# A transformer block with a 16,384-expert layer: routing without casts and spread wider, GpSimd on a third of u's lower parts, and v's last two groups by column halves

## The chip, the cores and the metric

The kernel runs on one core of one Trainium2 chip, with its engines TensorE (PE), VectorE (DVE), ScalarE (ACT), GpSimd (POOL) and the DMA queues that SyncE (SP), ACT and POOL feed. The metric is the device time of one execution in microseconds (us). The median of three executions is 2597.5 us (2593.54 to 2606.66). Lower is better.

## The reference, cut to what matters

One block of a diffusion transformer on 256 tokens of width 2048 in float32: a token mixer (differential attention and gated linear attention, in the first half of the time, which the diff does not touch), and then the PEER layer, a sparse layer of 16,384 experts:

```python
def peer_ffn(h, wq, keys, u, v):
    q = (h @ wq).reshape(B, T, PEER_HEADS, 2, PEER_DQ // 2)             # 8 heads, 2 halves of 128
    s = jnp.einsum('bthpd,hpkd->bthpk', q, keys)                        # 128 keys for each half
    s1, i1 = lax.top_k(s[..., 0, :], PEER_TOPK)                         # 16 best of each half
    s2, i2 = lax.top_k(s[..., 1, :], PEER_TOPK)
    cand = (s1[..., :, None] + s2[..., None, :]).reshape(B, T, PEER_HEADS, 256)
    cidx = (i1[..., :, None] * PEER_NKEYS + i2[..., None, :]).reshape(B, T, PEER_HEADS, 256)
    top_s, pos = lax.top_k(cand, PEER_TOPK)
    idx = jnp.take_along_axis(cidx, pos, axis=-1)
    g = jax.nn.softmax(top_s, axis=-1)
    ...
        act = jax.nn.gelu(jnp.einsum('pd,ped->pe', xb, u[ib]), approximate=False)
        return jnp.einsum('pe,ped->pd', act * gb, v[ib])
```

u and v are 16384 x 2048 tables (134 MB each in float32). The output is x plus a gate times this layer.

## The kernel before, in words

**Products.** TensorE multiplies in float32r, so that every float32 weight block of 128 x 1024 (0.524 MB by its shape) is split in two: `hi`, a rounded copy that ACT makes (L90, tile `whi`), and `lo`, the rest, a subtraction `raw - hi` (L92, tile `wlo`) that either DVE or POOL makes. The class `Stream` (object `W`) walks over one long list of blocks: SP loads them ahead into `wraw` buffers (L76), `split_to` makes `hi` and `lo` up to 3 blocks ahead of the products, and `W.share(s)` says for block `s` whether POOL makes `lo` (else DVE). Instructions of one engine run in the order in which they are written.

**Dense and sparse part of the PEER layer.** For 192 of the 256 tokens (TD) the layer is computed densely: all 128 groups of 128 experts are multiplied (u), a weight matrix `A` built from the routing masks out the experts that were not chosen, and a second pass multiplies by v. For the last 64 tokens (NS), 64 gathers of 128 rows of u (128 x 2048 float32, 1.05 MB by its shape), and later 64 of v, are fetched by indirect DMAs that POOL issues (L1163, tile `gat`, 2 buffers), and DVE multiplies them (L1170 with `hrow` in PSUM for u, L1185 for v).

**Jobs.** Everything beside the products is written as generators in lanes of `Jobs`. The product loops call `jobs.tick()`, and a generator that yields n goes on n ticks later. In the product with u (`experts_in`) a tick comes every four pairs of matmuls (a *pair* is L1219 with `hi` and L1220 with `lo`; a group of experts has 16 pairs, all of u has 2048), and a block is used up every 8 pairs. In the product with v a tick comes every 5 matmuls.

**The order of the stages that the diff touches.**
- *Queries* (w_q, 32 blocks, from 1151 us on): q = h @ wq, scores, and the job `route`. `route` runs 16 rounds (8 heads, 2 halves of the tokens); a round finds the 16 best of each half (`best16`: MAX, MAX_INDEX and MATCH_REPLACE on DVE), adds them to 256 candidates, finds the 16 best of these, and turns their positions back into expert numbers (L1070 to L1080). Its yields are 1, 1, 2, 1, 2, so a round takes 7 ticks. Seven rounds and a part of the eighth are written among the products of the queries, the rest among those of u.
- *u, routing* (from 1253 us): the rest of `route`, then `weigh` (softmax). POOL makes `lo` of three blocks in four.
- *u, gains*: the job `gains` builds `A` in 48 steps of 4 ticks. The lane `sparse` does one gather and one multiplication of an earlier gather every 6 ticks, from the start of `gains` on. DVE makes all `lo` (`W.share` is always false from here to the end). Finished groups are parked in DRAM, since `A` does not exist yet: 36 pairs of groups.
- *u, fetch*: the parked groups come back (SP, tile `back`, one every 3 ticks) and are multiplied into `A` by DVE (L1258); the rest of the groups go straight to `A` (L1248).
- *v* (from 1973 us): 128 groups of 20 matmuls, into PSUM tiles `ya[0..3]` (128 tokens) and `yb[0..3]` (64 tokens, two halves stacked). The last group finishes one column quarter n after the other, and each is at once turned into output: DVE multiplies and adds, TensorE folds `yb` with one more matmul (L1355) that waits for DVE, and SP stores.

Of the kernel before, what the change touches and what calls it, by code (L numbers as in the profile page):

```python
# [7 lines left out]
F32 = mybir.dt.float32  # L8
# [3 lines left out]
AF = mybir.ActivationFunctionType  # L12
OP = mybir.AluOpType
# [12 lines left out]
TD, NS = 192, 64  # L26
# [109 lines left out]
def block_kernel(ctx, tc, a, out):  # L136
# [15 lines left out]
    for m in range(16):  # L152
        if m + NGA < 16:
# [4 lines left out]
    on_pool |= set(range(len(blocks), len(blocks) + 32))  # L158
    blocks += ([a["w_q"][i] for i in (0, 2, 1, *range(3, 32))] + [a["u"][i] for i in range(256)]
               + [a["v_rows"][i * 128:(i + 1) * 128, q * 1024:(q + 1) * 1024] for i in range(128) for q in range(2)])  # L160
# [879 lines left out]

    def score(h, q):
# [10 lines left out]

    def route(h, s):
        for b in (1, 0):
            v = tk.tile([128, 2, 16], F32, name="v", bufs=2)
            iu = tk.tile([128, 2, 16], U32, name="iu", bufs=2)
            il = tk.tile([128, 2, 16], F32, name="il", bufs=2)
            for i in range(2):
                best16(v[:, i], iu[:, i], s[:, 2 * b + i])
                yield 1  # L1060
# [6 lines left out]
            yield 2  # L1067
            pu = tk.tile([128, 2, 16], U32, name="pu", bufs=2)
            pf = tk.tile([128, 2, 16], F32, name="pf", bufs=2)
            V.tensor_scalar(pu[:, 0], pos, 4, None, op0=OP.logical_shift_right)  # L1070
            V.tensor_scalar(pu[:, 1], pos, 15, None, op0=OP.bitwise_and)
            V.tensor_copy(pf, pu)
            S.activation(il, iu, AF.Copy)
            oh = tk.tile([128, 2, 16, 16], F32, name="oh", bufs=1)
            ohf = oh.rearrange("p i k a -> p (i k) a")
            V.tensor_tensor(ohf, pf.rearrange("p i k -> p (i k)")[:, :, None].to_broadcast([128, 32, 16]),
                            io16[:, None, :].to_broadcast([128, 32, 16]), OP.is_equal)
            yield 1
            V.tensor_tensor(oh, oh, il[:, :, None, :].to_broadcast([128, 2, 16, 16]), OP.mult)
            V.reduce_sum(I12[:, b, :, 16 * h:16 * h + 16], oh, axis=AX.X)  # L1080
            yield 2
# [68 lines left out]
    nwq = W.s  # L1150
# [15 lines left out]
    def sparse_in(pool, n, wait):  # L1166
        for j in range(64 + n):
# [5 lines left out]
            yield wait  # L1173
# [115 lines left out]
    with tc.tile_pool(name="gpool", bufs=1, side="right") as pool:  # L1289
        while A is None or any(jobs.lanes.get("gains", ())):  # L1290
            if A is None and not any(jobs.lanes.get("route", ())):
# [3 lines left out]
                jobs.add("sparse", sparse_in(spool, 2, 6))  # L1295
                W.share = lambda s: False
# [32 lines left out]

    part(0)  # L1330
    for i in range(128):
        if i % 2 == 0 and i + 2 < 128:
            part(i + 2)
        t = parts[i // 2 * 2][:, i % 2]
        h0, h1, hb = t[:, 0:128, 0], t[:, 0:128, 1], t[:, 128:TD].rearrange("p t i -> p (t i)")
        for n in range(4):
            if n % 2 == 0:
                hi, lo = W.next()
            c = slice((n % 2) * 512, (n % 2) * 512 + 512)
            first, last = i == 0, i == 127  # L1340
            PE.matmul(ya[n], h0, hi[:, c], start=first, stop=False)  # L1341
            PE.matmul(ya[n], h1, hi[:, c], start=False, stop=False)  # L1342
            PE.matmul(yb[n], hb, hi[:, c], start=first, stop=False)  # L1343
            PE.matmul(ya[n], h0, lo[:, c], start=False, stop=last)  # L1344
            PE.matmul(yb[n], hb, lo[:, c], start=False, stop=last)  # L1345
            jobs.tick()
            if last:
                d = slice(n * 512, n * 512 + 512)
                o = pool.tile([128, 512], F32, name="o", bufs=2)
                V.tensor_tensor(o, ya[n], g2r[:, d], OP.mult)  # L1350
                V.tensor_tensor(o, o, x2r[0][:, d], OP.add)
# [111 lines left out]
```

## Time and profile before

| | |
|---|---|
| Median of 3 executions | 2597.5 us |
| Profiled execution: its own time | 2595.49 us |
| Profiled execution: span from first to last instruction | 2593.7 us |
| Busy in the span: PE, DVE, ACT, POOL | 94%, 76%, 50%, 26% |
| DMA: mean rate over the span | 261 GB/s |
| Queries / product with u / product with v (us from the span's start) | 1151 to 1253 / 1253 to 1973 / 1973 to 2594 |

A busy TensorE only says that matmuls were in flight. The granted clock (PEclk) is a share of 2.4 GHz, and a stretch between 0.5 and 1 was run partly at 1.2 GHz. All times below are counted from the span's start.

### The profile page before, as it was taken

The page shows a single profiled execution, that of the slowest core. Times are in us where ns is not written, and L with a number is a line of the kernel's source. Part 1 is how long each engine was busy: PE and PEld are TensorE (multiplying, and loading weights), DVE is VectorE, ACT ScalarE, POOL GpSimd, SP SyncE. Part 2 cuts the span into 40 slices and gives each one's busy share as a digit, 9 for nine tenths or more (in the row PEclk, how much of TensorE's full clock was granted, in tenths as well). Part 3 has the DMA queues.
Part 4 walks back from the last instruction along what each step waited for, and adds up shares of the span by engine and source line. Part 5 has one row for each costly group of instructions (what it writes and reads, how often), then busy time and mean ns, then how long its engine had stood idle before and what let it go on. Part 6 is the DMA issues. An engine that isn't in the chain of part 4 may idle for free.

```text
span 2593.7 us, 39672 instructions
## 1 busy us (share of the span) xinstructions
PE 2434.1 (94%) x15236; PEld 2190.2 (84%) x15236; DVE 1974.8 (76%) x2609; ACT 1298.6 (50%) x1963; POOL 685.8 (26%) x334
## 2 busy tenths in 40 slices
PE   6799999999999999979779999999999999999998
PEld 3477888888899999979778999989998888888885
DVE  4868888577865665459996888889976888888765
ACT  5453444333344444443336999854554444444442
POOL 4541111212202342147444121222210332322100
PEclk8799999999999999989889999999999999999999
DMA  8665555366647776665456999999997999999973
GB/s 296 221 230 178 182 192 186 122 219 203 212 139 246 256 246 228 199 186 184 129 161 217 325 328 330 328 380 387 394 349 242 367 378 382 365 377 381 334 248 126
DMA packets 195406, 678.07 MB, mean 261 GB/s; under 512 B 21776, under 2 KB 53104, under 8 KB 178064
## 3 DMA queue, kind: packets, MB, share of 16 engines
q1 hardware_dynamic: 155232, 521.50, 58.2%
q0 software_dynamic: 19008, 137.44, 13.5%
q10 hardware_dynamic: 20976, 16.61, 2.1%
q8 instruction: 119, 1.95, 0.3%
q14 instruction: 71, 0.58, 0.1%
HBM read 660.44 MB, written 11.29 MB: 259 GB/s over the span
## 4 chain that ended last, share of the span: by engine, by line
PE 71%; DVE 17%; DMA 5%; issue 2%; ACT 2%; POOL 1%; SPq 0%; ACTq 0%; DVEq 0%; POOLq 0%
PE acc L1219 11%; PE acc L212 6%; PE acc L214 6%; PE acc L213 6%; PE acc L1220 5%; PE yb L1345 5%; PE ya L1341 5%; PE ya L1342 5%; PE ya L1344 5%; PE yb L1343 5%; DVE wlo L92 3%; DMA back<-park 3%; PE acc L411 2%; PE acc L413 2%; PE acc L414 2%
## 5 line engine op out<-in xcount | busy, mean ns | idle before, releaser
L92 DVE TENSOR_TENSOR wlo<-wraw,whi 128x1024 fp32r<-128x1024 f32 x678 | 855.9, 1282 | 286.6 <-ACT whi L90 283.7
L90 ACT ACTIVATE whi<-wraw 128x1024 fp32r<-128x1024 f32 x824 | 852.5, 1053 | 247.3 <-PE yb L1343 43.2
L1219 PE MATMUL acc<-H,whi 128*128 128x384 f32 x2048 | 617.3, 366 | 2.3 <-ACT whi L90 2.3
L92 POOL TENSOR_TENSOR wlo<-wraw,whi 128x1024 fp32r<-128x1024 f32 x146 | 372.9, 2562 | 818.0 <-ACT whi L90 781.2
L1220 PE MATMUL acc<-H,wlo 128*128 128x192 f32 x2048 | 524.6, 256 | 43.0 <-DVE wlo L92 42.8
L1220 PEld LDWEIGHTS acc<-H,wlo 128*128 128x128 f32 x2048 | 397.8, 194 | 50.6 <-DVE wlo L92 50.3
L1219 PEld LDWEIGHTS acc<-H,whi 128*128 128x128 f32 x2048 | 391.6, 191 | 2.5 <-ACT whi L90 2.5
L212 PE MATMUL acc<-H,whi 128*128 128x256 f32 (+1 forms) x1248 | 376.9, 302 | 1.4 <-ACT whi L90 1.4
L214 PE MATMUL acc<-H,wlo 128*128 128x256 f32 (+1 forms) x1248 | 372.0, 298 | 1.2 <-DVE wlo L92 0.8
L213 PE MATMUL acc<-H,whi 128*128 128x256 f32 (+1 forms) x1248 | 371.3, 297 | 0.0
L212 PEld LDWEIGHTS acc<-H,whi 128*128 128x128 f32 x1248 | 239.1, 192 | 19.6 <-issue 11.4
L214 PEld LDWEIGHTS acc<-H,wlo 128*128 128x128 f32 x1248 | 239.1, 192 | 9.0 <-DVE wlo L92 1.4
L213 PEld LDWEIGHTS acc<-H,whi 128*128 128x128 f32 x1248 | 239.1, 192 | 5.8
L1163 POOL DMA_INDIRECT gat<-v_rows,sidx x64 | 131.6, 2057 | 383.6 <-DVE ys L1185 292.8
L1163 POOL DMA_INDIRECT gat<-u_rows,sidx x64 | 106.5, 1664 | 398.6 <-DVE gat L1170 396.0
L387 DVE SCALAR_TENSOR_TENSOR a<-a,cb 128x1024 f32<-128x1024 f32 x128 | 193.0, 1512 | 22.8 <-DMA a<-ada 22.7
L1341 PE MATMUL ya<-whi,as 128*128 128x512 f32 x512 | 203.6, 398 | 2.0 <-DMA wraw<-v_rows 2.0
L1345 PE MATMUL yb<-wlo,as 128*128 128x512 f32 x512 | 205.2, 401 | 0.0
L1342 PE MATMUL ya<-whi,as 128*128 128x512 f32 x512 | 203.7, 398 | 0.0
L1344 PE MATMUL ya<-wlo,as 128*128 128x512 f32 x512 | 202.5, 396 | 0.0
L1343 PE MATMUL yb<-whi,as 128*128 128x512 f32 x512 | 201.6, 394 | 0.0
L1185 DVE SCALAR_TENSOR_TENSOR ys<-gat,sg,ys 128x2048 f32<-128x2048 f32 x63 | 148.0, 2349 | 25.2 <-DMA gat<-v_rows,sidx 25.0
(329 smaller groups left out, 4165.3 us busy)
## 6 DMA issues: line engine op xcount, KB each, us to landing
wraw<-u SPq DMA_DIRECT2D x256, 512.0 KB, 6.4
wraw<-v_rows SPq DMA_DIRECT2D x256, 512.0 KB, 7.5
wraw<-w_a SPq DMA_DIRECT2D x162, 512.0 KB, 3.9
a<-ada SPq DMA_DIRECT2D x128, 512.0 KB, 5.0
wraw<-ada SPq DMA_DIRECT2D x64, 512.0 KB, 4.6
wraw<-w_br SPq DMA_DIRECT2D x32, 512.0 KB, 4.4
wraw<-w_o SPq DMA_DIRECT2D x32, 512.0 KB, 4.3
wraw<-w_q SPq DMA_DIRECT2D x32, 512.0 KB, 4.0
```

Source lines behind the costliest of these rows:

```text
L90: nc.scalar.activation(hi, r, AF.Copy)
L92: e.tensor_tensor(lo, r, hi.bitcast(F32), OP.subtract)
L212: PE.matmul(acc[:, :n], hi[:, c], mh, start=(k == 0), stop=False)
L213: PE.matmul(acc[:, :n], hi[:, c], ml, start=False, stop=False)
L214: PE.matmul(acc[:, :n], lo[:, c], mh, start=False, stop=(k == nk - 1))
L1219: PE.matmul(acc[:, 0:2 * TD], hi[:, c], H2[:, k], start=(k == 0), stop=(k == KT - 1), skip_group_check=True)
L1220: PE.matmul(acc[:, 0:TD], lo[:, c], H2[:, k, 0:TD], start=False, stop=(k == KT - 1), skip_group_check=True)
L1341: PE.matmul(ya[n], h0, hi[:, c], start=first, stop=False)
L1342: PE.matmul(ya[n], h1, hi[:, c], start=False, stop=False)
L1343: PE.matmul(yb[n], hb, hi[:, c], start=first, stop=False)
L1344: PE.matmul(ya[n], h0, lo[:, c], start=False, stop=last)
L1345: PE.matmul(yb[n], hb, lo[:, c], start=False, stop=last)
```

## The change

1. `route` compares and multiplies the unsigned integers directly: the copy to float on DVE (`pf`, L1072) and the one on ACT (`il`, L1073) are gone.
2. `route` yields `pace(2), pace(2), pace(3), pace(2), pace(2)`. Among the products of the queries that is 1, 1, 2, 1, 1 (6 ticks a round), among those of u 2, 2, 3, 2, 2 (11 ticks).
3. From the start of `gains` to the end of u, POOL makes `lo` of every third block.
4. The gathers of u come every 8 ticks while `gains` runs and every 4 ticks after it, instead of every 6.
5. In v, the order inside a quarter is `yb` first, and the last two groups run as column half 0 of both, then column half 1 of both. The output of `yb` becomes a job, so that its folding matmul is written one quarter later, with stores on ACT's queue and four `o` buffers instead of two.

```diff
-               + [a["v_rows"][i * 128:(i + 1) * 128, q * 1024:(q + 1) * 1024] for i in range(128) for q in range(2)])
+    vorder = [(i, q) for i in range(126) for q in range(2)] + [(i, q) for q in range(2) for i in (126, 127)]
+               + [a["v_rows"][i * 128:(i + 1) * 128, q * 1024:(q + 1) * 1024] for i, q in vorder])
...
+    nwq = [1 << 30]
+    pace = lambda n: n if W.i >= nwq[0] else max(1, n * 2 // 3)
...
     def route(h, s):
         for b in (1, 0):
-            il = tk.tile([128, 2, 16], F32, name="il", bufs=2)
             for i in range(2):
                 best16(v[:, i], iu[:, i], s[:, 2 * b + i])
-                yield 1
+                yield pace(2)
...
-            yield 2
+            yield pace(3)
             pu = tk.tile([128, 2, 16], U32, name="pu", bufs=2)
-            pf = tk.tile([128, 2, 16], F32, name="pf", bufs=2)
...
-            V.tensor_copy(pf, pu)
-            S.activation(il, iu, AF.Copy)
...
-            V.tensor_tensor(ohf, pf.rearrange("p i k -> p (i k)")[:, :, None].to_broadcast([128, 32, 16]),
+            V.tensor_tensor(ohf, pu.rearrange("p i k -> p (i k)")[:, :, None].to_broadcast([128, 32, 16]),
                             io16[:, None, :].to_broadcast([128, 32, 16]), OP.is_equal)
-            yield 1
-            V.tensor_tensor(oh, oh, il[:, :, None, :].to_broadcast([128, 2, 16, 16]), OP.mult)
+            yield pace(2)
+            V.tensor_tensor(oh, oh, iu[:, :, None, :].to_broadcast([128, 2, 16, 16]), OP.mult)
             V.reduce_sum(I12[:, b, :, 16 * h:16 * h + 16], oh, axis=AX.X)
-            yield 2
+            yield pace(2)
...
-    nwq = W.s
+    nwq[0] = W.i
...
-                jobs.add("sparse", sparse_in(spool, 2, 6))
-                W.share = lambda s: False
+                jobs.add("sparse", sparse_in(spool, 2, lambda: 8 if any(jobs.lanes["gains"]) else 4))
+                W.share = lambda s: s % 3 == 0 and s < nwq[0] + 256
...
+    def rows_a(n):
+        d = slice(n * 512, n * 512 + 512)
+        o = pool.tile([128, 512], F32, name="o", bufs=4)
+        V.tensor_tensor(o, ya[n], g2r[:, d], OP.mult)
+        V.tensor_tensor(o, o, x2r[0][:, d], OP.add)
+        nc.sync.dma_start(out[0:128, d], o)
+    def rows_b(n):
+        d = slice(n * 512, n * 512 + 512)
+        o = pool.tile([128, 512], F32, name="o", bufs=4)
+        V.tensor_tensor(o, yb[n], g2r[:, d], OP.mult)
+        yield 1
+        PE.matmul(yb[n][0:NS], IJ, o, start=True, stop=True, skip_group_check=True)
+        V.tensor_tensor(o[0:NS], yb[n][0:NS], x2r[1][0:NS, d], OP.add)
+        nc.scalar.dma_start(out[128:TD, d], o[0:NS])
+        yield
...
-    for i in range(128):
+    for i, q in vorder:
...
+        for n in (2 * q, 2 * q + 1):
+            PE.matmul(yb[n], hb, hi[:, c], start=first, stop=False)
+            PE.matmul(yb[n], hb, lo[:, c], start=False, stop=last)
             PE.matmul(ya[n], h0, hi[:, c], start=first, stop=False)
             PE.matmul(ya[n], h1, hi[:, c], start=False, stop=False)
-            PE.matmul(yb[n], hb, hi[:, c], start=first, stop=False)
             PE.matmul(ya[n], h0, lo[:, c], start=False, stop=last)
-            PE.matmul(yb[n], hb, lo[:, c], start=False, stop=last)
             jobs.tick()
             if last:
...
+                jobs.add("end", rows_b(n), 0)
+                jobs.tick(0)
+                rows_a(n)
```

How the instructions stand in a row, at three places. First DVE in the last round of `route`, within the product with u; names are those of the tiles above. Before:

```order
L1035 MAX top<-cand 128x8
L1036 MAX_INDEX pos<-top,cand 128x8
L1037 MATCH_REPLACE cand<-top,cand 128x256
L1038 MAX top<-cand 128x8
L1039 MAX_INDEX pos<-top,cand 128x8
L1070 TENSOR_SCALAR pu<-pos 128x16
L1071 TENSOR_SCALAR pu<-pos 128x16
L1072 CAST pf<-pu 128x32
L1076 TENSOR_TENSOR oh<-pf,iota 128x512
L1079 TENSOR_TENSOR oh<-oh,il 128x512
L1080 TENSOR_REDUCE I_11241<-oh 128x2x16
```

Of the change:

```order
L1040 MAX top<-cand 128x8
L1041 MAX_INDEX pos<-top,cand 128x8
L92 TENSOR_TENSOR wlo<-wraw,whi 128x1024
L1075 TENSOR_SCALAR pu<-pos 128x16
L1076 TENSOR_SCALAR pu<-pos 128x16
L1079 TENSOR_TENSOR oh<-pu,iota 128x512
L1082 TENSOR_TENSOR oh<-oh,iu 128x512
L1083 TENSOR_REDUCE I_11241<-oh 128x2x16
```

The cast is gone, and a lower part now stands inside the round, since a round stretches over more products.

Second, POOL from the middle of `gains` to after its end. Before, the 64 gathers of u are one row with nothing between them; of the change (the place where two gathers in a row first occur is the end of `gains`):

```order
L1166 DMA gat<-u_rows,sidx 128x2048
L92 TENSOR_TENSOR wlo<-wraw,whi 128x1024 x2
L1166 DMA gat<-u_rows,sidx 128x2048 x2
L92 TENSOR_TENSOR wlo<-wraw,whi 128x1024
L1166 DMA gat<-u_rows,sidx 128x2048 x2
L92 TENSOR_TENSOR wlo<-wraw,whi 128x1024
L1166 DMA gat<-u_rows,sidx 128x2048 x2
L92 TENSOR_TENSOR wlo<-wraw,whi 128x1024
L1166 DMA gat<-u_rows,sidx 128x2048
```

Each subtraction on POOL now stands behind a gather that waits for a buffer, and three gathers come for every two subtractions. Third, the end of TensorE's program (tiles with their numbers: `ya_20223` and `yb_20227` are quarter 2, `ya_20224` and `yb_20228` quarter 3, `yb_20226` quarter 1), of the change:

```order
L1347 MATMUL yb_20226<-o,IJ 64x512
L1362 MATMUL yb_20228<-whi,as 128x512
L1363 MATMUL yb_20228<-wlo,as 128x512
L1364 MATMUL ya_20224<-whi,as 128x512
L1365 MATMUL ya_20224<-whi,as 128x512
L1366 MATMUL ya_20224<-wlo,as 128x512
L1347 MATMUL yb_20227<-o,IJ 64x512
L1347 MATMUL yb_20228<-o,IJ 64x512
```

Before, the folding matmul of a quarter (L1355) stands directly behind the five products of that quarter. Now the one of quarter 1 stands before the last products, and only those of quarters 2 and 3 stand behind them.

Counted in the program's order, the stages of u lie at these pairs of the 2048: `route` ends at pair 236 before and 321 after; `gains` starts at 317 and 405 and its last step is at 1085 and 1181; parked groups are 36 and 38 pairs of groups; the last gathered rows are multiplied at 1866 and 1821. Before, 16 - 7 = 9 rounds end within u; after, 8.

## Rows read from the trace of the kernel before

**Rows 1.** The page: the span and the busy time of each engine with its share and instructions.

```profile
span 2593.7 us, 39672 instructions
PE 2434.1 (94%) x15236; PEld 2190.2 (84%) x15236; DVE 1974.8 (76%) x2609; ACT 1298.6 (50%) x1963; POOL 685.8 (26%) x334
```

**Rows 2.** The product with u in nine stretches that are cut at pairs 100, 236, 317, 405, 1085, 1181, 1569 and 1821; only line L1219, the first matmul of a pair. Columns: stretch, its length, busy time of TensorE and of its weight loads on that line with the count, granted clock, share of the DMA engines, rate in GB/s.

```profile
1253.10:1311.10 58.00, 34.04 (x100) 21.49 (x101) 0.79 0.40 134
1311.10:1368.10 57.00, 44.37 (x138) 28.30 (x137) 0.88 0.53 162
1368.10:1401.80 33.70, 26.14 (x83) 16.53 (x82) 0.90 0.59 178
1401.80:1432.00 30.20, 26.22 (x89) 16.50 (x89) 1.00 0.84 291
1432.00:1673.40 241.40, 204.15 (x682) 128.09 (x681) 1.00 0.91 327
1673.40:1703.60 30.20, 28.02 (x98) 18.01 (x97) 1.00 1.00 371
1703.60:1829.70 126.10, 114.37 (x389) 72.90 (x389) 1.00 1.01 384
1829.70:1905.10 75.40, 73.67 (x254) 47.33 (x253) 1.00 1.01 395
1905.10:1971.60 66.50, 65.96 (x228) 42.44 (x227) 1.00 0.83 283
```

**Rows 3.** All engines in the routing stretch, in the stretch of `gains` and in the one of the fetch: length, then busy time (and count) of PE, PE's weight loads, DVE, ACT and POOL, then clock, DMA share and rate.

```profile
1253.00:1384.00 131.00, 93.16 (x565) 89.91 (x563) 124.96 (x292) 48.39 (x79) 64.82 (x26) 0.86 0.47 149
...
1432.00:1673.40 241.40, 241.34 (x1750) 239.73 (x1749) 208.18 (x316) 222.81 (x428) 48.69 (x29) 1.00 0.91 327
...
1703.60:1829.70 126.10, 118.66 (x802) 114.20 (x801) 111.16 (x125) 62.58 (x98) 26.85 (x16) 1.00 1.01 384
```

**Rows 4.** Who waited for whom from 1253 to 1384 us: engine, line, what it waited for, us in total, times, longest.

```profile
ACT il L1073 <- DVE iu L1039: 49.8, 8, 10.7
...
PE acc L1220 <- DVE wlo L92: 29.5, 7, 9.1
```

**Rows 5.** From the timeline: one round of `route` on DVE beside subtractions of POOL, and where the next begins and ends (start, us, engine, line, operation).

```profile
1292.22 7.00 POOL L92 TENSOR_TENSOR wlo<-wraw,whi 128x1024 fp32r<-128x1024 f32 x3 [4.57 <-ACT whi L90]
...
1292.42 2.23 DVE L1070 TENSOR_SCALAR pu<-pos 128x16 uint32<-128x16 uint32 x1
...
1294.76 2.20 DVE L1072 CAST pf<-pu 128x32 f32<-128x32 uint32 x1
1297.00 2.77 DVE L1076 TENSOR_TENSOR oh<-pf,iota 128x512 f32<-128x512 f32 x1
1299.88 0.69 DVE L1079 TENSOR_TENSOR oh<-oh,il 128x512 f32<-128x512 f32 x1
...
1302.34 0.29 DVE L1035 MAX8 v<-s 128x8 f32<-128x128 f32 x1
...
1309.00 0.18 DVE L1072 CAST pf<-pu 128x32 f32<-128x32 uint32 x1
...
1311.34 1.22 DVE L92 TENSOR_TENSOR wlo<-wraw,whi 128x1024 fp32r<-128x1024 f32 x1
```

**Rows 6.** Subtractions (L92) from 1253.1 to 1384: length, busy time and count of DVE and of POOL, clock, DMA.

```profile
1253.10:1384.00 130.90, 16.72 (x10) 64.82 (x26) 0.86 0.47 149
```

**Rows 7.** A DVE instruction with one operand in PSUM (`sp`), its durations in ns as least/median/most over all of them; then DVE in one stretch of the timeline in which POOL subtracts from 333.43 to 335.82.

```profile
L515 DVE TENSOR_TENSOR al<-sp,ah x8: 684/686/690, 220.8 to 482.2; 128x512 fp32r<-128x512 f32 x8
...
333.16 0.69 DVE L515 TENSOR_TENSOR al<-sp,ah 128x512 fp32r<-128x512 f32 x1
333.76 3.15 DVE L387 SCALAR_TENSOR_TENSOR a<-a,cb 128x1024 f32<-128x1024 f32 x1
```

**Rows 8.** The first and the last of four gathers of u on POOL that follow each other in the timeline (in brackets the idle time before and what ended it), and from the views of the tiles `gat` (1830 to 1905 us) and `back` the DVE instructions on them and the time from issue to landing.

```profile
1852.41 1.68 POOL L1163 DMA_INDIRECT gat<-u_rows,sidx  x1 [4.40 <-DVE gat L1170]
...
1871.21 1.68 POOL L1163 DMA_INDIRECT gat<-u_rows,sidx  x1 [4.52 <-DVE gat L1170]
...
L1170 DVE SCALAR_TENSOR_TENSOR gat<-gat,hrow x12: 2280/2282/2287, 1829.0 to 1904.0; 128x2048 f32<-128x2048 f32 x12
...
DMA to landing us min/median/max: 8.4/9.4/10.0
...
L1258 DVE TENSOR_TENSOR A<-A,back x36: 551/559/561, 1707.8 to 1842.2; 128x384 f32<-128x384 f32 x36
```

**Rows 9.** The end of the timeline: TensorE around the four folding matmuls (L1355), the last DVE instruction and the last store.

```profile
2569.81 0.39 PE L1344 MATMUL ya<-wlo,as 128*128 128x512 f32 x1
2570.04 0.40 PE L1345 MATMUL yb<-wlo,as 128*128 128x512 f32 x1
...
2572.32 1.07 PE L1355 MATMUL yb<-o,IJ 128*64 128x512 f32 x2 [1.88 <-DVE o L1354]
...
2588.08 1.29 PE L1355 MATMUL yb<-o,IJ 128*64 128x512 f32 x2 [1.93 <-DVE o L1354]
2589.41 0.68 DVE L1356 TENSOR_TENSOR o<-yb,gat 64x512 f32<-64x512 f32 x1 [1.38 <-PE yb L1355]
2590.12 0.47 SPq L1357 DMA_DIRECT2D out<-o  x1
```

More of the change, by code (lines that the diff above doesn't have):

```diff
@@ L1172, in sparse_in @@
                 gather(pool, a["u_rows"], j, n)
-            yield wait
+            yield wait()
         S.activation(dot, dot, AF.Gelu)
@@ L1328, in part @@
         split(t[:, :, :, 0], t[:, :, :, 1], A[:, i:i + 2])
+    def rows_a(n):
[13 more added lines that the diff above has]
+        yield
     part(0)
-    for i in range(128):
-        if i % 2 == 0 and i + 2 < 128:
+    for i, q in vorder:
+        if i % 2 == 0 and q == 0 and i + 2 < 128:
             part(i + 2)
@@ L1335, in block_kernel @@
         h0, h1, hb = t[:, 0:128, 0], t[:, 0:128, 1], t[:, 128:TD].rearrange("p t i -> p (t i)")
-        for n in range(4):
-            if n % 2 == 0:
-                hi, lo = W.next()
+        hi, lo = W.next()
+        for n in (2 * q, 2 * q + 1):
             c = slice((n % 2) * 512, (n % 2) * 512 + 512)
             first, last = i == 0, i == 127
+            PE.matmul(yb[n], hb, hi[:, c], start=first, stop=False)
+            PE.matmul(yb[n], hb, lo[:, c], start=False, stop=last)
             PE.matmul(ya[n], h0, hi[:, c], start=first, stop=False)
             PE.matmul(ya[n], h1, hi[:, c], start=False, stop=False)
-            PE.matmul(yb[n], hb, hi[:, c], start=first, stop=False)
             PE.matmul(ya[n], h0, lo[:, c], start=False, stop=last)
-            PE.matmul(yb[n], hb, lo[:, c], start=False, stop=last)
             jobs.tick()
             if last:
[L1348 to L1351, printed above, removed]
-                nc.sync.dma_start(out[0:128, d], o)
-                o = pool.tile([128, 512], F32, name="o", bufs=2)
-                V.tensor_tensor(o, yb[n], g2r[:, d], OP.mult)
-                PE.matmul(yb[n][0:NS], IJ, o, start=True, stop=True, skip_group_check=True)
-                V.tensor_tensor(o[0:NS], yb[n][0:NS], x2r[1][0:NS, d], OP.add)
-                nc.sync.dma_start(out[128:TD, d], o[0:NS])
+                jobs.add("end", rows_b(n), 0)
+                jobs.tick(0)
+                rows_a(n)
     jobs.drain()
```

## Prediction

> **What bounds the kernel now.** I read the page first: TensorE has work in flight for 94% of the span [rows 1], so only stretches in which it waits or runs slowly can be won, and any stretch in which it is made to wait is lost. The diff leaves the first 1151 us alone. The second view cuts the product with u at counted pairs [rows 2]; the reader should divide length by pairs. In the last stretch nothing disturbs it: 66.5 us for 227 pairs, 0.293 us a pair at a granted clock of 1.00, the 2.4 GHz level. During `gains` it is 241.4 / 680 = 0.355, with TensorE busy for 241.34 of 241.40 us [rows 3]. It is slow in two places. The first 317 pairs take 148.7 us (0.47 each), at a clock of 0.79 to 0.90, a mixture of the two levels, where TensorE had stood idle. The fetch stretch takes 126.1 / 388 = 0.325 while the DMA engines are full (share 1.01 at 384 GB/s).
>
> The routing stretch is DVE's: busy 125.0 of 131 us [rows 3], and TensorE waits for lower parts that stand behind routing work in DVE's row [rows 4]. ACT waits 49.8 us there for DVE's indices (`il`), which delays the upper parts that POOL needs. In the product with v TensorE's matmuls follow each other every 0.23 us [rows 9] until the last group, where the folding matmuls wait about 2 us each for DVE.
>
> **Step 1, routing (pairs 0 to 405).** What DVE does alone: the round from 1302.34 to 1311.34 ran undisturbed in 9.0 us, of it 0.2 for the cast [rows 5]. Beside POOL the same instructions grow: three subtractions of POOL run back to back for 7.00 us, and in that time `pu`, the cast and the comparison take 2.23, 2.20 and 2.77 us, against 0.18 for the undisturbed cast and 0.69 for the same-sized multiply [rows 5]. Before, 9 rounds at 9.0 and 10 subtractions at 1.14 (they follow each other that closely) make 92 us of work, and DVE was busy 125: 33 us of waiting, half of POOL's 64.8 [rows 3, 6].
>
> After, 8 rounds are left in u, at 8.8 us; 321 pairs use 40 blocks, so 10 subtractions on DVE and 30 on POOL, at 2.4 us (7.00 / 3 = 2.33 back to back, 64.8 / 26 = 2.49 over the stretch), 72 us. DVE: 8 x 8.8 + 11.4 = 82, plus half of 72, plus the 6 us that it idled before: 124 us. Lower bound, TensorE's own pace: 321 x 0.293 = 94. Upper bound, DVE waits for all that POOL runs: 82 + 72 = 154. I take the measured half. The next 84 pairs (`weigh`) go at about 0.30: 25. So pair 405 is reached after 149 us instead of 178.9: **-30 us** (bounds -60 and 0). The cast on ACT costs nothing by itself (ACT busy 48 of 131 us), but its removal lets ACT run ahead of DVE, which helps POOL and not DVE. The eighth round that moves into the queries lies under TensorE's work there, as the other seven; if that cover were gone it would cost 9 to 14 us at the start of u, where DVE takes it over.
>
> **Step 2, gains (pairs 405 to 1181).** TensorE is full here [rows 3], so taking a third of the subtractions off DVE (busy 208 of 241 us) buys nothing, and neither do fewer gathers. 776 pairs at 0.355 are 275 us, against 271.6 before for the same pair numbers, since `gains` itself has moved: **+4 us**. POOL's subtractions could hold up DVE (`og`, the lower parts). Two things cover it: DVE has a seventh of its time free and gets more, and its longest instruction, L1170 with 2.28 us, reads `hrow` in PSUM. No row shows that instruction beside a POOL subtraction; the nearest, L515 with an operand in PSUM, keeps 684 to 690 ns in all its eight runs, while the next DVE instruction, with both operands in SBUF, took 3.15 us [rows 7]. I take nothing for it; without that cover each gather would add up to 2.4 us.
>
> **Step 3, the gathers after gains (pairs 1181 to 1821).** Fewer gathers in `gains` means more afterwards: 24 steps of 8 ticks, so 40 are left, one every 4 ticks, in 160 ticks. By the products alone that would be 640 x 0.293 = 188 us, 4.7 us a gather. Two other limits lie above it. *Bytes*: 160 ticks of u at 0.262 MB, 40 gathers at 1.05 and 38 parked pairs at 0.197 are 91 MB, at 384 to 395 GB/s [rows 2] 231 to 238 us. *The two buffers*: a gather is issued when the one before the last has been multiplied, lands 9.4 us later, and needs 2.28 us on DVE [rows 8]; where DVE came right behind the landing, POOL issued four from 1852.41 to 1871.21, one every 6.27 us [rows 8]. 40 of them are 251 us; one and a half periods less, as two are on their way at the start, 242. DVE needs about 4.9 us a gather (2.3 + 1.33 x 1.2 + 1.33 x 0.56 + 0.28), so it is not the limit unless POOL holds it. What waits behind a late gather is everything in DVE's row: lower parts, hence TensorE, and POOL's next subtraction, which stands behind the next gather. I take 242 against 201.5 us before: **+40 us** (bounds +27, the bytes at 400 GB/s; +58, 6.5 us a gather). The last 227 pairs keep their 66.5.
>
> **Step 4, the end.** Before, quarter 0 is done at 2570.2 and 15 matmuls remain, 3.5 us; the last store is issued at 2590.1 and the span ends 3.6 us later. Now two folding matmuls (1.07 each) lie between products, which end near 2575.9. Behind them DVE does six instructions of 0.69 us, of which the last two enclose the last fold (1.3): DVE ends near 2581.6, the span near 2585.2, so **-8.5 us** (bounds -6 and -10) [rows 9]. The new order inside a quarter moves `lo` two matmuls (0.46 us) earlier; it is made up to three blocks ahead, so I put it at nothing.
>
> **Sum.** 2593.7 - 30 + 4 + 40 - 8.5 = 2599.2 us of span, and 1.8 us outside it as before: 2601 us. The profiled time before (2595.5) lies 2 us under the median.
>
> **A rule beside the rows.** The Trainium skill, SBUF — State Buffer, section "SBUF: two separate sides", says that DVE and GpSimd share a pair of ports under an exclusive lock: a DVE instruction with two SBUF inputs waits for the whole of a GpSimd instruction that reads SBUF, and the other way round. The trace agrees, 2.77 instead of 0.69 us [rows 5]. By that rule alone, taken to its end, the 67 subtractions that steps 2 and 3 move to POOL take 67 x 1.2 = 82 us off DVE and hold it up for 67 x 2.4 = 161 us; at the measured half they hold it for 80, and DVE has gained nothing. That is the second rival below, which is priced from rows.
>
> **Rivals.**
> - *The routing runs at TensorE's pace, and the gathers only cost their bytes* (faster). For it: with `il` gone the upper parts come evenly, so POOL no longer subtracts in threes just when DVE reaches `pu` and the comparison; a round has 11 ticks x 1.17 = 12.9 us of products to hide in and needs 8.8 plus 1.4. Against it: POOL's 72 us and those instructions of DVE that rows 5 and 6 show to exclude them (8 x 2 x 0.69 and 10 x 1.14, 22 us) already add up to 94. Full price: -60 + 4 + 27 - 8.5 = -37, 2558 us; half way on both, 2575. Chance 0.32.
> - *POOL holds DVE up more than before* (slower). For it: three blocks in four are POOL's and more blocks pass while routing runs, and its third in the fetch stretch meets DVE's `A` products, all with both operands in SBUF. If DVE waits for all of POOL's time in routing (step 1: 0) and a gather takes 6.5 us (+58), the sum is +54, 2649 us. It decides (slower by over 0.5%) from about 63% of POOL's 72 us on, at a gather loop as in step 3. Against it: half was measured, in a stretch with `pf` and the bunching. Chance 0.28.
> - *POOL's third does nothing and steps 1 and 3 cancel*: this is the forecast, chance 0.40.
>
> **Numbers.** A change of about 0.5% (13 us) is what a measurement of this kernel can tell from none. The forecast is 2601 us, its own range 2585 to 2611. Both rivals hold over a quarter, so the range reaches half into each: 2570 to 2628. Faster 0.32, same 0.40, slower 0.28.
>
> **What would show it.** Step 1: pair 405 near 1402 us, DVE still over 90% busy in routing, and no wait of ACT for `iu`. Step 2: 0.355 us a pair in `gains` with DVE freer. Step 3: gathers issued every 6 to 6.5 us behind the end of `gains`, DMA share near 1, DVE idle before L1173 for the gather's DMA, and TensorE behind DVE's lower parts. Step 4: 9 to 10 us from the last product to the end. I am wrong if a gather comes every 5 us, if DVE's instructions with two SBUF operands are no longer stretched in routing, or if TensorE waits for lower parts in `gains`.

## The result, and the profile after

The changed kernel takes 2615.0 us (median of 5; 2609.4 to 2618.2), the kernel before 2595.0 in the same comparison: 1.0067 times as long, 95% interval 1.0043 to 1.0091, so slower by about two thirds of a per cent, with a lower end just inside the half per cent that counted as no change. The forecast was 2601 us and no change. The time lies inside the whole range (2570 to 2628), but outside the range of the likeliest case (2585 to 2611).

The page after, its line of the span and its engines' busy time (before: [rows 1]):

```profile
span 2613.2 us, 39725 instructions
...
PE 2445.1 (94%) x15236; PEld 2204.1 (84%) x15236; DVE 1953.5 (75%) x2516; ACT 1296.2 (50%) x1947; POOL 861.9 (33%) x411
```

POOL has 176 us more, DVE only 21 us less, although its 93 instructions fewer are 16 casts and 77 subtractions of 1.2 us (those that POOL has more): most of what was taken off DVE came back as longer instructions. The product with u, cut at the pairs 321, 405, 1085, 1181 and 1821 (columns as in [rows 2]; only the first matmul of a pair, now L1222):

```profile
1249.10:1368.50 119.40, 99.62 (x321) 63.61 (x322) 0.94 0.58 192
1368.50:1396.30 27.80, 24.93 (x86) 15.83 (x85) 1.00 0.70 229
1396.30:1649.90 253.60, 204.35 (x681) 128.00 (x681) 1.00 0.81 280
1649.90:1685.90 36.00, 28.85 (x97) 18.08 (x97) 1.00 0.81 278
1685.90:1931.00 245.10, 204.32 (x642) 130.11 (x641) 0.92 0.99 374
1931.00:1997.40 66.40, 65.86 (x227) 42.36 (x227) 1.00 0.73 234
```

Lengths by the same pair numbers, before and after, from these rows and [rows 2]:

| stretch | before | after | measured | predicted |
|---|---|---|---|---|
| queries end (pair 0 starts) | 1253.1 | 1249.1 | -4.0 | 0 |
| routing, pairs 0 to 405 | 178.9 | 147.2 | -31.7 | -30 |
| gains, 405 to 1181 | 271.6 | 289.6 | **+18.0** | **+4** |
| after gains, 1181 to 1821 | 201.5 | 245.1 | +43.6 | +40 |
| 1821 to the end of u | 66.5 | 66.4 | 0 | 0 |
| v and the end | 622.1 | 615.8 | -6.3 | -8.5 |

The sum is +19.5 us, which is the difference of the two profiled executions (2615.0 and 2595.5). Of the 14 us by which the forecast was short, 14 stand in one row: `gains`. The other deviations (-4.0, -1.7, +3.6 and +2.2) cancel by luck. Nothing can be read from the -4.0 of the queries: kernels below that are the same up to there end them anywhere between 1244.3 and 1252.3.

All engines in that stretch (columns as in [rows 3]), then TensorE's waits in it:

```profile
1396.30:1685.90 289.60, 277.36 (x1987) 272.38 (x1986) 217.36 (x300) 251.55 (x483) 110.01 (x58) 1.00 0.81 280
```

```profile
PE acc L1223 <- POOL wlo L92: 6.9, 8, 0.9
PE sp L1281 <- DVE og L1276: 5.4, 15, 0.5
```

Before, TensorE waited for next to nothing while `gains` ran [rows 3]. Now it waits for POOL's lower parts and for DVE's `og`, at a clock of 1.00. DVE is busy for 75% of the stretch, so this is no lack of time on DVE. Its groups of instructions in the stretch, with their forms (line, engine, operation, tiles, form, count | busy us, mean ns):

```profile
L92 DVE TENSOR_TENSOR wlo<-wraw,whi 128x1024 fp32r<-128x1024 f32 x64 | 96.4, 1506 | 71.9 <-ACT whi L90 68.2 <-ACT A L1288 3.7
L1276 DVE TENSOR_SCALAR og<-iota,I1T,GT 128x128 f32<-128x128 f32 x192 | 78.8, 474 | 4.9 <-ACT GT L1122 4.9
L1173 DVE SCALAR_TENSOR_TENSOR gat<-gat,hrow 128x2048 f32<-128x2048 f32 x22 | 50.2, 2283 | 0.0
```

The gather's multiply L1173 keeps its 2.28 us [rows 8], as the forecast had assumed for it. The other two have grown: a subtraction from 1224 ns (its mean in this stretch of the kernel before) to 1506, an `og` from 351 to 474. The timeline shows which ones (start, us, engine, line; in brackets the idle time before and what ended it; other instructions between these lines are left out):

```profile
1461.20 2.28 DVE L1173 SCALAR_TENSOR_TENSOR gat<-gat,hrow 128x2048 f32<-128x2048 f32 x1
1463.76 0.95 POOL L1166 DMA_INDIRECT gat<-u_rows,sidx  x1 [7.91 <-PE acc L1223]
1464.73 3.48 DVE L92 TENSOR_TENSOR wlo<-wraw,whi 128x1024 fp32r<-128x1024 f32 x1 [1.24 <-ACT whi L90]
1464.74 2.39 POOL L92 TENSOR_TENSOR wlo<-wraw,whi 128x1024 fp32r<-128x1024 f32 x1
1467.18 0.36 PE L1223 MATMUL acc<-H,wlo 128*128 128x192 f32 x1 [0.86 <-POOL wlo L92]
...
1471.31 2.29 DVE L1173 SCALAR_TENSOR_TENSOR gat<-gat,hrow 128x2048 f32<-128x2048 f32 x1
1471.93 2.42 POOL L92 TENSOR_TENSOR wlo<-wraw,whi 128x1024 fp32r<-128x1024 f32 x1 [4.81 <-ACT whi L90]
...
1488.52 3.92 DVE L1276 TENSOR_SCALAR og<-iota,I1T,GT 128x128 f32<-128x128 f32 x4
1489.45 2.40 POOL L92 TENSOR_TENSOR wlo<-wraw,whi 128x1024 fp32r<-128x1024 f32 x1
1491.99 1.00 PE L1281 MATMUL sp<-og,oh 128*128 128x128 f32 x6 [0.50 <-DVE og L1276]
```

POOL's subtraction always takes 2.4 us. Beside L1173 (1471.93) neither notices the other. Beside DVE's own subtraction (1464.73) that one takes 3.48 instead of 1.2 us, beside the four `og` (1488.52) they take 3.92 instead of 1.11, and each time TensorE waits. The two waits differ. At 1491.99 it is for the lengthened `og`. At 1467.18 it is for POOL's own part, which is not longer than elsewhere but late: it stands in POOL's row right behind a gather that had waited for L1173 to free its buffer. (The gather's bracket names a product that ended at the same moment; by the records every such gather starts 0.27 us after L1173's sum is read out.) All eight waits for POOL's part in this stretch are of that kind. The waits are 12.3 of the 18.7 us by which the stretch is longer than the 270.9 us of the kernels below; the rest is in TensorE's own busy time (277.4 for 270.9), which I read as matmuls in flight behind a late one; no run shows that. Since gathers come every four blocks of u and POOL subtracts every third, the place moves on from one subtraction to the next and repeats after twelve blocks: in 36 us one falls beside L1173, one beside nothing, one beside DVE's subtraction, one beside `og`. Summed over the stretch, 11.8 of POOL's 79.3 us of subtraction lie under L1173, 19.8 under DVE's own and 21.6 under `og` (added up from the records).

The stretch behind `gains` went as described, with one addition. TensorE's and DVE's waits in it, and the gathers:

```profile
DVE gat L1173 <- DMA gat<-u_rows,sidx: 29.4, 14, 5.0
PE acc L1223 <- POOL wlo L92: 29.1, 13, 3.1
...
PE acc L1223 <- DVE wlo L92: 5.1, 5, 1.4
```

```profile
L1166 POOL DMA_INDIRECT gat<-u_rows,sidx x40: 940/1030/1762, 1690.5 to 1924.4; - x40
...
DMA to landing us min/median/max: 6.0/8.2/9.3
```

40 gathers from 1690.5 to 1924.4, one every 6.0 us, DMA engines full at 374 GB/s. The lower parts for which TensorE waits are mostly POOL's, not DVE's: they stand behind a gather that waits for its buffer.

### The profile page after: what moved, and what is told of

The parts are those of the page before. It is cut to its first block, busy times and chain, and to the rows that moved or that the text cites. A ratio compares the mean times of both kernels' runs of the same rounds, so it can differ in the third digit from the quotient of the medians.

```text
span 2613.2 us, 39725 instructions
## 1 busy us (share of the span) xinstructions
PE 2445.1 (94%) x15236; PEld 2204.1 (84%) x15236; DVE 1953.5 (75%) x2516; ACT 1296.2 (50%) x1947; POOL 861.9 (33%) x411
## 5 line engine op out<-in xcount | busy, mean ns | idle before, releaser
L92 DVE TENSOR_TENSOR wlo<-wraw,whi 128x1024 fp32r<-128x1024 f32 x601 | 796.0, 1345 | 313.4 <-ACT whi L90 309.0
L92 POOL TENSOR_TENSOR wlo<-wraw,whi 128x1024 fp32r<-128x1024 f32 x223 | 567.4, 2552 | 915.7 <-ACT whi L90 886.1
L1222 PE MATMUL acc<-H,whi 128*128 128x384 f32 x2048 | 628.3, 370 | 0.0
L1223 PE MATMUL acc<-H,wlo 128*128 128x192 f32 x2048 | 530.3, 259 | 58.9 <-POOL wlo L92 36.0
L1223 PEld LDWEIGHTS acc<-H,wlo 128*128 128x128 f32 x2048 | 404.0, 197 | 68.2 <-POOL wlo L92 41.3
L1222 PEld LDWEIGHTS acc<-H,whi 128*128 128x128 f32 x2048 | 398.1, 194 | 0.0
L216 PEld LDWEIGHTS acc<-H,wlo 128*128 128x128 f32 x1248 | 239.8, 192 | 9.2 <-DVE wlo L92 1.2
L1188 DVE SCALAR_TENSOR_TENSOR ys<-gat,sg,ys 128x2048 f32<-128x2048 f32 x63 | 148.0, 2349 | 28.5 <-DMA gat<-v_rows,sidx 28.4
L1173 DVE SCALAR_TENSOR_TENSOR gat<-gat,hrow 128x2048 f32<-128x2048 f32 x64 | 146.0, 2282 | 30.9 <-DMA gat<-u_rows,sidx 30.9
```

The source lines that it names most:

```text
L92: e.tensor_tensor(lo, r, hi.bitcast(F32), OP.subtract)
L216: PE.matmul(acc[:, :n], lo[:, c], mh, start=False, stop=(k == nk - 1))
L1222: PE.matmul(acc[:, 0:2 * TD], hi[:, c], H2[:, k], start=(k == 0), stop=(k == KT - 1), skip_group_check=True)
L1223: PE.matmul(acc[:, 0:TD], lo[:, c], H2[:, k, 0:TD], start=False, stop=(k == KT - 1), skip_group_check=True)
```

## The experiments

Stretches are given as routing (pair 0 to 405), gains (405 to 1181) and behind gains (1181 to 1821), in us. What the next table takes from the traces is worked out as in the table above.

| kernel | median, us | times before | routing | gains | behind gains |
|---|---|---|---|---|---|
| after | 2615.0 | 1.0067 | 147.2 | 289.6 | 245.1 |
| without part 3 | 2587.3 | 0.9960 | 145.4 | 270.9 | 235.2 |
| without part 4 | 2567.1 | 0.9877 | 145.5 | 270.9 | 213.7 |
| without both | 2559.0 | 0.9850 | 147.1 | 273.6 | 201.6 |
| part 5 alone | 2590.4 | 0.9968 | 179.9 | 271.6 | 204.4 |

### The parts apart

Without POOL's third in u (part 3):

```diff
-                W.share = lambda s: s % 3 == 0 and s < nwq[0] + 256
+                W.share = lambda s: False
```

> The change without its part 3: DVE makes every lower part again from the start of gains on; routing, gathers every 8 and 4 ticks and the new end stay. Theory A (each part acts in its own stretch: POOL's third costs the 14 us by which gains came out longer, the late gathers cost the stretch from pair 1181 to 1821): gains falls back to 0.355 us a pair, the stretch from pair 1181 to 1821 stays at 235 to 245 us, and the time is near 2601 us, 14 under the change. Rival B (in the last stretch it is POOL's subtractions, standing behind gathers that wait for a buffer, that hold TensorE: 29 us of waits on them in the changed kernel): that stretch falls to about 215 us too, and the time is near 2572 us.

Measured 2587.3 us, 0.9960 (0.9942 to 0.9977), in the middle between the two times. The lengths decide for A: the stretch behind gains is 235.2 us, at the lower end of A's range, and B's 215 did not come. A's time was too high since gains gave back 18.7 us instead of 14, and the stretch behind them 9.9. With the gathers of the changed kernel, but no subtraction on POOL in u's later part, gains fall to 270.9 us. Behind gains 235.2 remain:

```profile
1664.30:1899.50 235.20, 201.92 (x1322) 191.25 (x1321) 207.95 (x216) 104.52 (x162) 54.48 (x40) 0.99 1.01 387
```

The DMA share is 1.01 at 387 GB/s, and the forecast's 91 MB in 235.2 us are 387 GB/s: the bytes account for the length. With POOL's third it is 245.1, 10 us more. All engines there, and TensorE's largest wait without the third:

```profile
1685.90:1931.00 245.10, 210.34 (x1323) 205.09 (x1322) 213.92 (x192) 104.34 (x162) 120.12 (x67) 0.92 0.99 374
```

```profile
PE acc L1223 <- DVE wlo L92: 32.8, 34, 2.4
```

TensorE waits about as long in both, 34.6 us with the third and 33.2 without. What differs is its busy time, 210.3 us for 201.9, and its granted clock, 0.92 for 0.99: worked out from these two shares, some 39 us of the stretch ran at 1.2 GHz, against some 5 without the third. With the third the waits are fewer and longer (13 for POOL's part, up to 3.1 us, and 5 for DVE's). That the longer waits bring the clock down is likely, but no run tests it.

Without the new pace of the gathers (part 4):

```diff
-                jobs.add("sparse", sparse_in(spool, 2, lambda: 8 if any(jobs.lanes["gains"]) else 4))
+                jobs.add("sparse", sparse_in(spool, 2, lambda: 6))
```

> The change without its part 4: a gather every 6 ticks throughout; POOL keeps its third. Theory A: the stretch from pair 1181 to 1821 falls from 245 to about 205 us, gains keeps its extra 14 us or a few more, since more gathers fall into it; time near 2577 us. Rival B: POOL's subtractions still stand behind waiting gathers, the stretch stays above 225 us, time near 2598 us.

Measured 2567.1 us, 0.9877 (0.9845 to 0.9909), below both. The stretch behind gains, 213.7 us, lies between the two theories. The gains do not keep the extra time that A gave them: they take 270.9 us again, although POOL subtracts every third block:

```profile
1397.60:1668.50 270.90, 270.90 (x1987) 270.90 (x1986) 199.52 (x316) 251.78 (x483) 118.94 (x66) 1.00 0.93 327
```

Without both (both edits together):

> The change without its parts 3 and 4: routing without casts and spread wider, and the new end, alone. Theory A: pair 405 near 147 us after the start of u as in the change, gains at 0.355 us a pair, the stretch from pair 1181 to 1821 near 203 us; 36 to 40 us faster than the kernel before, near 2558 us. If the gain of the routing is given back later (the gathers now begin 88 pairs later and end later, and the fetch meets them), the time would be near 2580 us.

Measured 2559.0 us, 0.9850 (0.9824 to 0.9875): as expected, and parts 1, 2 and 5 alone are 1.5% faster than before. On this base part 3 alone costs 8.1 us (2567.1), part 4 alone 28.3 (2587.3), both together 56.0. That is 19.6 more than the sum of the two, and the table says where: the gains are slow only when both are there.

Part 5 alone, on the kernel before:

> The kernel before with part 5 alone (order inside a quarter, column halves of the last two groups, output of yb as a job, stores on ACT's queue). Theory: 6 to 7 us faster than before, as the trace of the change shows from the start of v to the end, near 2588.5 us. Rival: the new order inside a quarter also changed the product with v itself, then the difference would lie before the last group.

Measured 2590.4 us, 0.9968 (0.9956 to 0.9980): 6.7 us less than the 2597.1 of before, as in the trace of the change (-6.3). In its trace the last two groups and the output take 22.1 us instead of 29.3, while v before them is 2.0 us longer: the gain is that of the end, and this trace shows none from the new order inside a quarter.

### The place of POOL's subtraction

If it is the place, a shift of it must change the gains at the same amount of work. First the kernel without part 4, whose gathers come every three blocks, in step with POOL's third: there 46.3 of POOL's 79.5 us lay under L1173. The shift is one block:

```diff
-                W.share = lambda s: s % 3 == 0 and s < nwq[0] + 256
+                W.share = lambda s: s % 3 == 1 and s < nwq[0] + 256
```

> Like the kernel whose gathers keep their six ticks (2567.1 us), only that GpSimd takes the blocks of u with s % 3 == 1 instead of 0: as many blocks, as many gathers, each of GpSimd's subtractions one block later against the gather. Theory A (what matters is which operation of VectorE GpSimd's subtraction lies beside): in the changed kernel the subtractions that fall one block after the gather's multiply lie beside VectorE's own subtraction, 19.2 of 21.6 us of them, so here some 32 of them do, each stretching one by about 2.4 us, 70 us on a VectorE that is busy 94% of the gains: that stretch becomes 285 to 300 us instead of 270.9, the time 2580 to 2605. Rival B (the load counts, not the place): gains 271 us, time 2563 to 2571.

Measured 2610.7 us, 1.0052 (1.0032 to 1.0072): 44 us slower than the same kernel unshifted. Gains take 316.7 us instead of 270.9: theory B falls, and it is more than theory A said. (The 94% in this expectation is ACT's share of the stretch; DVE was busy for 199.5 of 270.9 us, 74%.)

```profile
1396.40:1713.10 316.70, 282.60 (x1987) 272.89 (x1986) 267.19 (x316) 251.46 (x483) 111.70 (x66) 1.00 0.83 282
```

```profile
PE sp L1281 <- DVE og L1276: 21.2, 30, 1.2
PE acc L1223 <- POOL wlo L92: 12.9, 15, 0.9
```

DVE executes the same 316 instructions as above and is busy 267 us instead of 200; POOL's 78.5 us now lie under DVE's subtraction (37.6) and `og` (35.5).

Then the changed kernel, with gathers every four blocks, and POOL taking every fourth block in three of the four places:

```diff
-                W.share = lambda s: s % 3 == 0 and s < nwq[0] + 256
+                W.share = lambda s: s % 4 == 0 and s < nwq[0] + 256
```

> The changed kernel, with GpSimd taking the blocks of u with s % 4 == 0 instead of s % 3 == 0, so that its subtractions keep one place against the gathers, which come every four blocks. Theory A: it is the place beside the gather's multiply L1173 (in the changed kernel the subtractions of these blocks lay under L1173 for 11.8 of their 19.3 us); gains 270 to 276 us instead of 289.6, although VectorE subtracts three blocks of four instead of two of three; the last stretch 235 to 250 us as before; time 2590 to 2607. Rival B (load): with more blocks on VectorE and the gathers as in the changed kernel the gains take 285 us or more, time 2610 to 2620.

> The same with s % 4 == 1: theory A: each of GpSimd's some 24 subtractions of the gains lies beside VectorE's own subtraction (19.2 of 21.6 us in the changed kernel) and stretches it by up to 2.4 us, some 50 us: gains 285 to 300 us, 10 us or more above those of s % 4 == 0. Rival B (load): gains within 3 us of those of s % 4 == 0.

> The same with s % 4 == 2: theory A: each of GpSimd's subtractions lies beside the multiply by the gate L1276 (16.8 of 19.2 us in the changed kernel), a tensor_scalar of 0.33 us that then takes 2.4 us or more: some 50 us more on VectorE, and the sum behind it late: gains 283 to 300 us. Rival B (load): gains within 3 us of those of s % 4 == 0.

| s % 4 | median, us | times before (95%) | gains | POOL's subtractions lie under |
|---|---|---|---|---|
| 0 | 2590.1 | 0.9986 (0.9971 to 1.0002) | 271.0 | L1173, 43.7 of 60.2 us |
| 1 | 2633.7 | 1.0152 (1.0129 to 1.0174) | 306.1 | DVE's L92, 54.3 of 59.8 |
| 2 | 2610.0 | 1.0055 (1.0038 to 1.0072) | 289.1 | `og`, 52.7 of 59.9 |

The stretch of gains in the three, in this order, and the waits of TensorE in the second and third (in the first there are none):

```profile
1390.60:1661.60 271.00, 271.00 (x1988) 271.00 (x1986) 191.26 (x308) 251.67 (x483) 85.08 (x50) 1.00 0.85 298
```

```profile
1391.50:1697.60 306.10, 282.23 (x1987) 272.22 (x1986) 234.92 (x308) 251.22 (x483) 85.30 (x50) 1.00 0.80 265
```

```profile
1389.70:1678.80 289.10, 278.20 (x1987) 274.00 (x1986) 245.33 (x308) 251.51 (x483) 101.70 (x50) 1.00 0.80 280
```

```profile
PE acc L1223 <- POOL wlo L92: 18.9, 22, 0.9
PE sp L1281 <- DVE og L1276: 5.0, 22, 0.2
```

```profile
PE sp L1281 <- DVE og L1276: 10.9, 22, 0.5
```

308 instructions on DVE and 50 on POOL in each, and 35 us between the best and the worst place. The load theory expected them within 3 us of one another, and falls. The place in POOL's row decides it, too. In the second kernel POOL's subtraction stands right behind a gather that waits for L1173 to free its buffer, so it cannot run beside L1173 and starts with DVE's next subtraction (other instructions between are left out):

```profile
1471.54 2.28 DVE L1173 SCALAR_TENSOR_TENSOR gat<-gat,hrow 128x2048 f32<-128x2048 f32 x1
1474.10 0.95 POOL L1166 DMA_INDIRECT gat<-u_rows,sidx  x1 [9.43 <-PE acc L1223]
1475.07 3.48 DVE L92 TENSOR_TENSOR wlo<-wraw,whi 128x1024 fp32r<-128x1024 f32 x1 [1.24 <-ACT whi L90]
1475.07 2.38 POOL L92 TENSOR_TENSOR wlo<-wraw,whi 128x1024 fp32r<-128x1024 f32 x1
1477.51 0.36 PE L1223 MATMUL acc<-H,wlo 128*128 128x192 f32 x1 [0.86 <-POOL wlo L92]
```

In the first kernel it stands ahead of the gather and starts as soon as its upper part is there:

```profile
1473.40 2.41 POOL L92 TENSOR_TENSOR wlo<-wraw,whi 128x1024 fp32r<-128x1024 f32 x1 [7.66 <-ACT whi L90]
1475.96 0.95 POOL L1166 DMA_INDIRECT gat<-u_rows,sidx  x1 [0.16 <-issue]
```

The costs differ as well: 35 us for 22 meetings beside DVE's subtraction, 18 us for 22 beside `og`, although DVE loses more in the second case (over the shortest of each kind, 64 us in `og` against 52 in L92, added up from the records). So it isn't DVE's lost time that counts, but what TensorE waits for. In the third kernel that is the lengthened `og` alone, so there the 18 us are the price of holding DVE. In the second, 18.9 of the 23.9 us of waits are for POOL's part, which takes its usual 2.38 us and starts 2.66 us after its upper part is ready (0.77 in the third kernel, 0.08 in the first; from the records). That is lateness in POOL's row, not DVE being held. The same holds for phase_1 (12.9 us for POOL's part). So two mechanisms are at work: a held DVE instruction that TensorE takes at once, and a subtraction of POOL stuck behind a waiting gather. No run has one in the second place without the other, so how the 35 us split is open.

### Routing: casts, pace and POOL's share

All three start from the kernel without parts 3 and 4 (2559.0 us). First the old yields with the casts removed, then the new yields with the casts kept:

```diff
-                yield pace(2)
+                yield 1
...
-            yield pace(3)
+            yield 2
```

> Against the kernel without parts 3 and 4 (2559.0 us, pair 405 reached 147.1 us after pair 0; before 178.9): the casts stay away, the old yields of route (1, 1, 2, 1, 2) come back. Theory C (the casts: il makes ACT wait for VectorE, so the upper parts and GpSimd's subtractions come in threes, and VectorE's casts are held up): pair 405 after 147 to 155 us, time 2559 to 2567. Theory P (the pace: a round spread over more products, and one round more among the queries): 168 to 179 us, time 2580 to 2591. In between, both.

> The other half: new yields, but il on ACT and pf on VectorE are cast as before. Theory C: pair 405 after 168 to 179 us, time 2580 to 2591. Theory P: 147 to 155 us, 2559 to 2567.

Without the pace 2575.5 us (median of three; a fourth execution took 10,833 us and is left out), 0.9913 (0.9883 to 0.9944); with the pace and the casts 2568.5 us, 0.9904 (0.9877 to 0.9931). With the casts kept the queries end 9 us later than in the base, of which 6.9 are one wait of TensorE for ACT, and their routing is 140.8 us long; so the point at which pair 405 starts is compared: 1434.0 us with neither (part 5 alone), 1423.0 with the casts removed, 1402.1 with the pace, 1399.4 with both. The pace gives 32 of the 35 us by itself. The casts alone give 11, and 3 on top of the pace. Theory P holds for most of it: routing without the pace (169.5 us) lies within its bounds, and the two times miss them by 4.5 and 1.5 us, towards C; the 140.8 us with the pace and the casts lie under P's 147 to 155, behind queries that end 9 us later. TensorE's waits for DVE's lower parts in routing are 17.0 us in the changed kernel and here, without the pace, 30.6 (before, up to 1384 us, 29.5 [rows 4]):

```profile
PE acc L1223 <- DVE wlo L92: 30.6, 6, 7.1
```

Then the share of POOL:

```diff
-    W.share = lambda s: s % 4 != 0
+    W.share = lambda s: s % 2 != 0
```

> The kernel without parts 3 and 4, in which GpSimd takes every second block during routing instead of three of four (also in the weighing behind it): about 10 more subtractions on VectorE up to pair 321 (12 us) and 10 fewer on GpSimd (25 us). If GpSimd holds VectorE up for half of its time, as the prediction's step 1 took it, the two cancel: pair 405 after 145 to 149 us (147.1), time 2557 to 2561. If VectorE waits for all of GpSimd's time: 134 to 137 us, time about 2547. If hardly for any: 157 to 160 us, about 2570.

Measured 2557.6 us, 0.9849 (0.9826 to 0.9873), routing 145.9 us: the two cancel. First routing up to pair 321 here, then in the changed kernel:

```profile
1250.10:1370.30 120.20, 103.39 (x665) 100.84 (x663) 114.46 (x270) 54.52 (x82) 48.76 (x20) 0.93 0.56 190
```

```profile
1249.10:1368.50 119.40, 102.31 (x664) 100.26 (x663) 113.31 (x264) 54.53 (x82) 77.17 (x30) 0.94 0.58 192
```

POOL has ten subtractions fewer (28.4 us), DVE as many more at 1.2 us, and DVE is busy for 114.5 us instead of 113.3. So 28.4 us of POOL had cost DVE about 11, 0.4 of its time; the forecast had used 0.5.

## Why the prediction was right or wrong

**Step 1, right.** -31.7 us against -30. Two small misses cancel in it: up to pair 321 it took 4.6 us less, from there to pair 405 27.8 us instead of 25. DVE was said to work or wait 124 us up to pair 321; it took 119.4, of them 113.3 busy. Half of POOL's time was a little too much (0.4), and the share of POOL costs nothing either way. ACT's wait for `iu` is gone, as said, but the runs show that this and the casts are the small part: the pace, and the round that it moves into the queries, do it.

**Step 2, wrong, and it is the whole miss.** The step said that POOL's third buys nothing, which holds: 270.9 us without it and 270.9 with it in step. It also said that it costs nothing, under the cover that DVE has a seventh of its time free and that L1170 (now L1173) reads `hrow` in PSUM. The second half of the cover is confirmed: 2.28 us with and without a subtraction of POOL beside it. The first half is no cover. The free time of DVE is a mean, while an `og` has an instant at which TensorE takes it; 2.8 us at the wrong place is late although DVE idles a moment later. The step named `og` and the lower parts as what POOL could hold up, but did not ask which of them stand beside POOL's subtractions, nor when POOL's own part would come: that a subtraction stands behind a waiting gather is said in step 3, for the stretch behind gains alone. With gathers every four blocks and subtractions every three, half of POOL's subtractions meet an instruction that is held, and a quarter come late behind a gather. +4 should have been +18; against the 270.9 us the two mechanisms cost 18.7, of which 5.4 are waits for `og` and 6.9 waits for POOL's part. The sentence "or if TensorE waits for lower parts in `gains`" named the sign by which the forecast would fail, and it is the one that the trace shows.

**Step 3, right in its sum, by luck.** +43.6 against +40, a gather every 6.0 us. Without POOL's third the stretch takes 235.2 us at a DMA share of 1.01, which is the bytes, where I had taken 242 from the loop of the two buffers. The loop isn't excluded: each of the 40 gathers there still waits for its buffer, and with a landing of 8.7 us instead of 9.4 the loop's 6.27 us come to about 5.9, too. The other 10 us come with POOL's subtractions, for which I had put no time here; the rows show them in TensorE's busy time at a clock of 0.92, not in longer waits. Two errors of about the same size, then, in opposite directions (242 for 235, nothing for 10).

**Step 4, right in kind.** -6.3 us against -8.5; the lower bound of its range was 6. Around the end of the timeline (before: [rows 9]):

```profile
2602.86 0.40 PE L1366 MATMUL ya<-wlo,as 128*128 128x512 f32 x1
...
2607.11 1.97 PE L1347 MATMUL yb<-o,IJ 128*64 128x512 f32 x2 [1.44 <-DVE o L1345]
2609.12 0.68 DVE L1348 TENSOR_TENSOR o<-yb,gat 64x512 f32<-64x512 f32 x1 [2.06 <-PE yb L1347]
```

From the last product to DVE's last instruction 6.5 us, where 5.7 were forecast; the last fold takes 1.97 us where I had put 1.3. The other 1.5 us lie before it: the last product ends 605.5 us after the end of u, where the forecast's 2575.9 made it 604.

**The rivals.** The slow rival's verdict came, slower by over 0.5%, though not its 2649 us. It had half of the mechanism (POOL holds DVE up) in the wrong places: it put the loss into routing and into the gathers' period, and the loss came in `gains`. The fast rival's first half, routing at TensorE's own pace (94 us), did not come: 119.4 us, and TensorE still waits 17.0 us there. Its second half, the gathers at their bytes, is what is left without part 3, and its 2558 us is what parts 1, 2 and 5 give alone, but for another reason: there the gathers keep their old pace.

**The lock.** The Trainium skill, SBUF — State Buffer, section "SBUF: two separate sides", states it as an exclusive lock, not a bandwidth split: one of the two engines blocks for the whole of the other's instruction. The traces agree, 3.48 = 1.2 + 2.3 us for the subtraction above. They agree also in that L1173, with one operand outside SBUF, isn't held. My second rival took the rule "to its end", as 2.4 us for every subtraction; in the gains the runs show that DVE's instruction loses 2.3 to 2.8 us or nothing, by the place.

## What to carry to other kernels

When work goes to an engine that shares a lock with another, the question is not how much free time the other has, but which of its instructions run beside the moved one, and what the moved one stands behind in its own engine's row. Two periodic streams in step can be put so that their meeting costs nothing (271.0 us), 18 us or 35 (289.1, 306.1), and streams of different periods meet in every place in turn. Look for a long instruction that the lock doesn't touch, put the moved work in the row ahead of whatever waits for that instruction, and give both the same period. Before that, ask whether the moved work was on the path at all: here the version without parts 3 and 4 (2559.0 us, 0.985 of before) beats both kernels.

## What was not expected of the hardware

`og`, a tensor_scalar with one tensor operand and two scalars per partition, all in SBUF, is held by POOL's subtraction like an instruction with two tensors: 3.92 instead of 1.11 us for four. The prediction had named it as a candidate, without a row for it. POOL's subtraction itself takes 2.36 to 2.42 us in all these meetings, though spans on POOL are rough in this profile, so by these records DVE pays alone. The records also show that it does not take an earlier start of POOL: the held instruction ends 1.09 us after POOL's subtraction where it is a subtraction, and 0.09 us after it where it is an `og`, also where DVE's record starts first (by 0.1 us for a subtraction in phase_1, by 0.67 us for the held `og`). Why POOL wins there they don't show.
